# A two-layer decoder step: the first two product tiles grow with the loaded inputs

## The chip, the cores and the metric

The kernel runs on one core of one Trainium2 chip. The metric is device time in microseconds of one execution, as the median of several. Five engines matter: TensorE (PE, with its weight loads shown apart as PEld), VectorE (DVE), ScalarE (ACT), GpSimd (POOL) and SyncE (SP), which here only issues DMAs. A granted clock of 1.00 means that no throttle was recorded.

## The reference

One inference step of a decoder with two layers, for a prompt of 512 tokens with 16 learned tokens ahead of it and for 8 sequences of 8 new tokens: 592 columns of 1024 features, all in float32. The part that the change touches is the very first: the first layer's first RMSNorm and the first product of its feed-forward block.

```python
def rms_norm(x, g):
    y = xf * lax.rsqrt(jnp.mean(xf * xf, axis=-1, keepdims=True) + EPS)
    return (y * g.astype(jnp.float32)).astype(x.dtype)

def swiglu(h, w_gu, w_down):
    g, u = jnp.split(h @ w_gu, 2, axis=-1)
    return (jax.nn.silu(g) * u) @ w_down

def layer(x, lp, ...):
    x = x + 0.5 * swiglu(rms_norm(x, lp['norm_ffn1']), lp['ffn1_w_gu'], lp['ffn1_w_down'])
    m, ... = mixer(rms_norm(x, lp['norm_mix']), ...)      # SSD scan and stick-breaking attention
    x = x + m
    x = x + 0.5 * swiglu(rms_norm(x, lp['norm_ffn2']), lp['ffn2_w_gu'], lp['ffn2_w_down'])
```

`ffn1_w_gu` is 1024 x 5632 (2816 gate columns, then 2816 up columns).

## The kernel before

**How the work is tiled.** The residual stream lies feature by feature: eight tiles `X[0..7]` of 128 features x 592 tokens. A product tile is 128 output features x 592 tokens, held in a pair of PSUM banks of 296 columns each. Both operands are split into a high part of reduced width (float32r) and a low part that holds the rest: weights into `whi` and `wlo`, inputs into `XH` and `XL`. A product tile is then, for each of the eight input tiles and each half, three matmuls: high by high, high by low, low by high. That makes 8 x 2 x 3 = 48 matmuls of 128 x 296.

**The norm.** RMSNorm's factor depends on the token alone, so the gain goes into the split of the inputs (`norm_tile`: `XH = X * gain` on ACT, `XL = X * gain - XH` on DVE), and the factor `R` is multiplied in when a product tile is read from PSUM (`times_r`, L231). `R` needs the squares of all eight tiles. `factor` makes it in steps that run between the matmuls of `mm3`: it is a generator (`flow`), and `step`, called once after each matmul, moves it on by one. With the numbers (8, 0, 20) it lets 8 matmuls pass, puts in the token sums (matmuls of the squares with a column of ones, L476), makes the reciprocal root in small DVE operations, lets 20 more pass, and spreads the result over all partitions with ten small matmuls (L208). Until then `hold` is set, and finished product tiles wait in PSUM, listed in `wait_done`.

**The start.** `setup` loads constants and calls `load_x`. It loads the tokens as rows in two halves of 512 features, with the first weight block (`raw0`, four input tiles x 256 columns) between the halves. For each input tile k it transposes six pieces on PE into a pair of banks (`xps`, 400 and 192 columns), copies them to `X[k]` (400 columns on DVE, 192 on ACT), and calls `norm_tile`, which splits the tile and makes its square: even tiles on POOL, odd ones on ACT. The squares are added into one tile, save the last, on DVE or POOL. Then `ffn` calls `gemm` for two gate tiles, two up tiles, and so on. `gemm` loads weight blocks (`raw`, three buffers), splits each when its product is due (`split`: ACT for the high part, DVE for the low one; three buffers each), and calls `mm3`.

**PSUM.** There are eight banks: three tagged `g`, two `pm`, and one each of `sc`, `po`, `pw`. `bank` deals them out in a cycle, with `turn` as the counter; `WIDE` is g, pm, g, pm, g, sc, and so leaves room for three product tiles. `factor` uses `po` and `pw`.

**Order.** The program text gives priorities; a planner goes through it with modelled durations and writes the order of each engine's instructions, so an instruction that is ready can be put ahead of one that stands before it in the text. In the mixer, hand-written due times (`PRI`, `UNIT`) move groups of instructions further.

Of the kernel before, what the change touches and what calls it, by code (L numbers as in the profile page):

```python
# [8 lines left out]
F32 = mybir.dt.float32  # L9
# [3 lines left out]
AF = mybir.ActivationFunctionType  # L13
ALU = mybir.AluOpType
# [3 lines left out]
D = 1024  # L18
KD = 8
DFF = 2816  # L20
NTOK = 592
# [85 lines left out]
class Kern:  # L107
# [126 lines left out]
    def setup(self):  # L234
        nc, I = self.nc, self.I
        off, arr = self.CA
        w = arr.shape[1]
        call = self.call = self.cst([128, w], "call")
        nc.sync.dma_start(call[:, 0:129], I["c_const"][:, 0:129])
        for k, (o, n) in off.items():  # L240
            setattr(self, "c_" + k, call[:, o:o + n])
        self.ident = self.c_ident
        self.identr = self.cst([128, 128], "identr", F32R)
        nc.vector.tensor_copy(self.identr, self.ident)
        self.flows, self.hold, self.wait_done, self.gn, self.gl, self.gi = [], False, [], "", "", 0
        self.eps = self.cst([128, 1], "eps")
        nc.vector.memset(self.eps, 1e-6)
        self.XH, self.XL = [None] * KD, [None] * KD
        self.cols(0, 296)
        self.par = self.cst([128, 128], "par")  # L250
        self.pcol = {}
        self.params(0, ("norm_ffn1", "norm_mix", "norm_ffn2"))
        self.load_x()
        self.norm_end()

    def params(self, r0, names):

# [130 lines left out]
    def load_x(self):  # L388
        nc, I = self.nc, self.I
        self.xtiles()  # L390
        src = [(I["meta_tokens"], 16, 0)]
        xp = I["x_prompt"][0]
        for b in range(4):
            src.append((xp[b * 128:(b + 1) * 128, :], 128, 16 + 128 * b))
        src.append((I["x_sample"].rearrange("b t d -> (b t) d"), 64, 528))
        toks = [(self.kv.tile([128, 1024], F32, name="xt", tag="kn", bufs=6), n, c) for _, n, c in src]
        for h in range(2):
            for (t, n, _), (s, _, _) in zip(toks, src):
                nc.sync.dma_start(t[0:n, 512 * h:512 * h + 512], s[:, 512 * h:512 * h + 512])
            if h == 0:  # L400
                self.raw0 = self.raw(I["ffn1_w_gu"][0], 0, 4, 0, 256)
        for k in range(KD):
            ps = self.pair("xps")
            for t, n, c in toks:
                o = ps[0][:, c:c + n] if c < 400 else ps[1][:, c - 400:c - 400 + n]
                nc.tensor.transpose(o, t[0:n, k * 128:k * 128 + 128], self.ident[0:n, 0:n])
            nc.vector.tensor_copy(self.X[k][:, 0:400], ps[0][:, 0:400])
            nc.scalar.activation(self.X[k][:, 400:592], ps[1][:, 0:192], AF.Copy)
            if k == 0:
                self.split0 = self.split(self.raw0, 4, 0)  # L410
            self.norm_tile(k, "norm_ffn1", 0, nc.gpsimd if k in (1, 3, 5) else nc.vector,
                           None if k % 2 else nc.gpsimd)

    def store_y(self, h):

# [220 lines left out]
    def gemm(self, src, r0, nk, c0, XH, XL, done, wide=2, after=None):  # L636

        kcs = []
        k = 0
        while k < nk:  # L640
            n = min(4, nk - k)
            kcs.append((k, n))
            k += n
        raws = {}
        if self.gn != self.gl:
            self.gl, self.gi = self.gn, 0
        base = self.gi
        self.gi += wide

        def part(k, n, m, ps):  # L650
            if k not in raws:
                raws[k] = self.raw0 or self.raw(src, r0 + k * 128, n, c0, wide * 128)
                self.raw0 = None
            with self.ahead(None, base + m):
                hi, lo = self.split0 or self.split(raws[k], n, m)
                self.split0 = None
            self.mm3(ps, hi, lo, n, XH[k:], XL[k:], k == 0, k + n == nk, after)

        wait = self.wait_done
        for m in range(wide):  # L660
            ps = self.pair("g")
            for k, n in kcs:
                part(k, n, m, ps)
            wait.append((done, m, ps))
            if not self.hold:
                with self.ahead(None, base + m):
                    for f, i, p in wait:
                        f(i, p)
                wait.clear()
# [977 lines left out]
```

## Time and profile before

| | us |
|---|---|
| runs shown | 2679.93, 2688.82, 2701.83 |
| median | 2688.82 |
| profiled execution | 2681.37 |
| its span | 2679.6 |
| mean granted clock | 0.987 |

The profile is of one execution. Its page names, for each engine, busy time, share of the span and number of instructions; a chain of waits leads back from the last instruction to what released it at each step; a timeline lists instructions with start and duration in us, and in brackets how long the engine had been idle and what ended that. Groups are written "line engine operation out<-in shape xcount | busy us, mean ns of one | idle before". `g` is a product tile, `xps` the transposed inputs, `x` is `X`, `xh` and `xl` its parts, `raw` a weight block, `xt` a block of tokens as loaded, `sq` a square. Ends of matmuls are modelled, so the pace of PE is read from starts.

### The profile page before, as it was taken

To read this page: it belongs to the slowest core of one execution; us is meant where nothing else is said; L and a number is where in the kernel's file an instruction comes from. 1 tells how busy PE (TensorE), PEld (TensorE's weight loads), DVE (VectorE), ACT (ScalarE), POOL (GpSimd) and SP (SyncE) were. 2 spreads that over 40 slices of the span, in tenths; PEclk is the share of its full clock that TensorE was granted. 3 is DMA by queue.
4 is the path that set the end of the run, shared out by engine and by line. 5 is a ranking of instruction groups with operands and counts; after the bars stand their busy time and mean duration, and the time that the engine had idled before them with its cause. 6 is when DMAs were issued, how large, how long until landed. Compare 5 with 4: busy or idle time off the path is not lost.

```text
span 2679.6 us, 51326 instructions
## 1 busy us (share of the span) xinstructions
PE 2600.5 (97%) x21547; PEld 2466.6 (92%) x21547; DVE 1505.1 (56%) x3005; ACT 978.9 (37%) x1771; POOL 304.7 (11%) x288
## 2 busy tenths in 40 slices
PE   8999999999889999999999999999998899999999
PEld 7999999898657999999999999998886579999998
DVE  6434346397886743444554343465878957444444
ACT  3222224256564432222332222233566634223222
POOL 1000000034532100000000000001345411000000
PEclk9999999999989999999999999999998999999999
DMA  3232234467973222222222323244678731222222
GB/s 113 80 115 82 85 113 131 127 214 264 336 241 129 70 81 79 79 79 79 79 79 79 97 85 100 78 151 164 223 253 300 249 128 56 88 86 79 85 89 76
DMA packets 245112, 343.28 MB, mean 128 GB/s; under 512 B 32809, under 2 KB 196721, under 8 KB 244881
## 3 DMA queue, kind: packets, MB, share of 16 engines
q1 hardware_dynamic: 208016, 205.77, 24.7%
q0 software_dynamic: 36864, 134.23, 14.5%
q8 instruction: 169, 2.77, 0.4%
q14 instruction: 63, 0.51, 0.1%
HBM read 320.29 MB, written 19.66 MB: 127 GB/s over the span
## 4 chain that ended last, share of the span: by engine, by line
PE 84%; DVE 7%; issue 3%; ACT 3%; DMA 2%; POOL 1%; SPq 0%; DVEq 0%; POOLq 0%; ACTq 0%
PE g L605 72%; PE v L926 2%; DVE kt L1519 2%; PE po L211 1%; PE sc L211 1%; DMA v<-in_cache_v,vi 1%; DVE st L1298 1%; PE pw L476 1%; DMA kn<-in_cache_k,ki 1%; DVE pst L1298 1%; POOL v L1569 0%; PE z L208 0%; PE z L211 0%; DVE xl L447 0%; DVE wlo L596 0%
## 5 line engine op out<-in xcount | busy, mean ns | idle before, releaser
L605 PE MATMUL g<-xl,whi 128*128 128x296 f32 (+1 forms) x3392 | 1014.6, 299 | 2.7 <-DVE xl L447 2.7
L605 PE MATMUL g<-xh,wlo 128*128 128x296 f32 (+1 forms) x3392 | 1012.9, 299 | 2.0 <-DVE wlo L596 2.0
L605 PE MATMUL g<-xh,whi 128*128 128x296 f32 (+1 forms) x3392 | 1011.1, 299 | 1.5 <-DVE gs L231 1.2
L595 ACT ACTIVATE whi<-raw 128x512 fp32r<-128x512 f32 (+1 forms) x664 | 412.6, 622 | 1323.6 <-PE g L605 1240.5
L596 DVE TENSOR_TENSOR wlo<-raw,whi 128x512 fp32r<-128x512 f32 (+1 forms) x664 | 450.3, 678 | 582.8 <-ACT whi L595 529.7
L605 PEld LDWEIGHTS g<-xl,whi 128*128 128x128 f32 x3392 | 638.6, 188 | 5.6 <-DVE xl L447 3.6
L605 PEld LDWEIGHTS g<-xh,wlo 128*128 128x128 f32 x3392 | 638.7, 188 | 4.3 <-DVE wlo L596 2.5
L605 PEld LDWEIGHTS g<-xh,whi 128*128 128x128 f32 x3392 | 638.7, 188 | 4.0 <-DVE gs L231 1.4
L605 PE MATMUL g<-hl,whi 128*128 128x296 f32 (+1 forms) x1408 | 417.8, 297 | 0.0
L605 PE MATMUL g<-hh,wlo 128*128 128x296 f32 (+1 forms) x1408 | 417.6, 298 | 0.0
L605 PE MATMUL g<-hh,whi 128*128 128x296 f32 (+1 forms) x1408 | 416.7, 298 | 0.0
L1508 POOL DMA_INDIRECT kn<-in_cache_k,ki x128 | 128.3, 1003 | 1657.9 <-PE g L605 934.8
L605 PEld LDWEIGHTS g<-hl,whi 128*128 128x128 f32 x1408 | 265.2, 188 | 0.0
L605 PEld LDWEIGHTS g<-hh,wlo 128*128 128x128 f32 x1408 | 264.3, 188 | 0.0
L605 PEld LDWEIGHTS g<-hh,whi 128*128 128x128 f32 x1408 | 263.9, 188 | 0.0
L1519 DVE STREAM_TRANSPOSE kt<-kn 128x512 f32<-128x512 f32 x256 | 162.9, 681 | 27.7 <-PE sc L211 14.5
L704 DVE SCALAR_TENSOR_TENSOR x<-g,x 128x296 f32<-128x296 f32 (+1 forms) x192 | 88.1, 463 | 119.1 <-PE g L605 118.5
L1569 POOL DMA_INDIRECT v<-in_cache_v,vi x128 | 143.3, 1119 | 100.0 <-DVE kt L1519 36.1
L231 DVE TENSOR_TENSOR us<-g,R 128x296 f32<-128x296 f32 (+1 forms) x176 | 81.5, 464 | 129.1 <-PE g L605 129.0
L231 DVE TENSOR_TENSOR gs<-g,R 128x296 f32<-128x296 f32 (+1 forms) x176 | 80.6, 463 | 126.2 <-PE g L605 121.3
L691 ACT ACTIVATE hh<-us 128x592 fp32r<-128x592 f32 (+1 forms) x88 | 61.2, 696 | 64.3 <-DVE us L689 64.3
L605 PE MATMUL g<-mh,whi 128*128 128x296 f32 (+1 forms) x256 | 77.7, 312 | 2.4 <-ACT mh L1277 1.3
(372 smaller groups left out, 2838.8 us busy)
## 6 DMA issues: line engine op xcount, KB each, us to landing
raw<-in_ffn_w_gu SPq DMA_DIRECT2D x176, 512.0 KB
raw<-in_ffn_w_down SPq DMA_DIRECT2D x80, 512.0 KB
raw<-in_w_in SPq DMA_DIRECT2D x44, 512.0 KB
raw<-in_w_out SPq DMA_DIRECT2D x16, 512.0 KB
spill<-x SPq DMA_DIRECT2D x16, 296.0 KB
x<-spill SPq DMA_DIRECT2D x16, 296.0 KB
raw<-in_ffn_w_down SPq DMA_DIRECT2D x16, 256.0 KB
xt<-in_x_prompt SPq DMA_DIRECT2D x8, 256.0 KB
```

Of the source, the lines that this page charges most:

```text
L211: i = self.nc.tensor.matmul(*a, **k).ins
L231: self.nc.vector.tensor_tensor(tv[0:P, h, :], ps[h][0:P, 0:self.n], rv[0:P, h, :], ALU.mult)
L595: nc.scalar.activation(hi[:, 0:nk], s, AF.Copy)
L596: nc.vector.tensor_tensor(lo[:, 0:nk], s, hi[:, 0:nk].bitcast(F32), ALU.subtract)
L605: mm = nc.tensor.matmul(ps[h][:, 0:self.n], w[:, k, :], self.hv(x)[:, h, :], start=(first and k == 0 and i == 0), stop=(last and k == nk - ...
L691: nc.scalar.activation(hh[:, a:b], u[:, a:b], AF.Copy)
L704: nc.vector.scalar_tensor_tensor(v, p, 0.5, v, ALU.mult, ALU.add)
L926: nc.tensor.matmul(ps[c], x[:, t0:t0 + 128], w.rearrange("p x c -> p (x c)"), start=(k == 0 and i == 0), stop=(k == 7 and i == 2))
L1298: self.nc.vector.tensor_tensor_scan(sv, sv, self.zero[0:rows].to_broadcast([rows, b - a - 1]), 1.0, ALU.mult, ALU.add)
L1508: self.nc.gpsimd.indirect_dma_start(kn, None, self.kflat, bass.IndirectOffsetOnAxis(ap=self.kidx[self.l][:, s, 2 * i + u:2 * i + u + 1], a ...
L1519: self.nc.vector.transpose(kt[:, 2 * u:2 * u + 2].rearrange("p t h i -> p t (h i)"), kns[u][:, :, 256 * quad:256 * quad + 256])
L1569: self.nc.gpsimd.indirect_dma_start(v.rearrange("p k c -> p (k c)"), None, self.vflat, bass.IndirectOffsetOnAxis(ap=self.vidx[self.l][:, s ...
```

## The change

`load_x` builds the first two product tiles itself. It loads both weight blocks of the first gate tiles (`raws`), reserves their PSUM banks (`self.first`: a `pm` and a `g` bank each), and takes only `sc`, `po` and `pw` in turn for the transposed inputs. For each input tile it makes the high part on ACT from `X[k]`, the low part on DVE in two pieces (400 and 192 columns) with PSUM as its source instead of `X[k]`, and then the 12 matmuls of this input tile for both product tiles. The copy of the left 400 columns goes to ACT for odd tiles. Weights are split for both product tiles at once, before input tiles 0 and 4. The squares come after all of that, two on ACT and six on POOL; the sums on DVE gather five of them into the first, so that three square tiles go into the token sums instead of two. `turn` is set to 4. The first call of `gemm` finds the two tiles done and only lists them in `wait_done`; the counted steps of `factor` therefore begin in the third product tile.

```diff
@@ setup
         self.load_x()
-        self.norm_end()
@@ load_x
+        wgu = I["ffn1_w_gu"][0]
         for h in range(2):
             for (t, n, _), (s, _, _) in zip(toks, src):
                 nc.sync.dma_start(t[0:n, 512 * h:512 * h + 512], s[:, 512 * h:512 * h + 512])
             if h == 0:
-                self.raw0 = self.raw(I["ffn1_w_gu"][0], 0, 4, 0, 256)
+                raws = [self.raw(wgu, 0, 4, 0, 256)]
+        raws.append(self.raw(wgu, 512, 4, 0, 256))
+
+        self.first = [self.pair("g", ("g", "pm")) for _ in range(2)]
         for k in range(KD):
-            ps = self.pair("xps")
+            ps = self.pair("xps", ("sc", "po", "pw"))
             for t, n, c in toks:
                 o = ps[0][:, c:c + n] if c < 400 else ps[1][:, c - 400:c - 400 + n]
                 nc.tensor.transpose(o, t[0:n, k * 128:k * 128 + 128], self.ident[0:n, 0:n])
-            nc.vector.tensor_copy(self.X[k][:, 0:400], ps[0][:, 0:400])
-            nc.scalar.activation(self.X[k][:, 400:592], ps[1][:, 0:192], AF.Copy)
-            if k == 0:
-                self.split0 = self.split(self.raw0, 4, 0)
-            self.norm_tile(k, "norm_ffn1", 0, nc.gpsimd if k in (1, 3, 5) else nc.vector,
-                           None if k % 2 else nc.gpsimd)
+            x, gain = self.X[k], self.pcl("norm_ffn1", 0, k)
+            self.XH[k], self.XL[k] = self.half("xh"), self.half("xl")
+            if k % 2:
+                nc.scalar.activation(x[:, 0:400], ps[0][:, 0:400], AF.Copy)
+            else:
+                nc.vector.tensor_copy(x[:, 0:400], ps[0][:, 0:400])
+            nc.scalar.activation(x[:, 400:592], ps[1][:, 0:192], AF.Copy)
+            nc.scalar.activation(self.XH[k], x, AF.Copy, scale=gain)
+            for p, c, n in ((ps[0], 0, 400), (ps[1], 400, 192)):
+                nc.vector.scalar_tensor_tensor(self.XL[k][:, c:c + n], p[:, 0:n], gain,
+                                               self.XH[k][:, c:c + n].bitcast(F32), ALU.mult, ALU.subtract)
+            if k % 4 == 0:
+                w = [self.split(raws[k // 4], 4, m) for m in range(2)]
+            for m in range(2):
+                for h in range(2):
+                    for i, (u, v) in enumerate(((w[m][0], self.XH[k]), (w[m][0], self.XL[k]), (w[m][1], self.XH[k]))):
+                        nc.tensor.matmul(self.first[m][h][:, 0:self.n], u[:, k % 4, :], self.hv(v)[:, h, :],
+                                         start=(k == 0 and i == 0), stop=(k == KD - 1 and i == 2))
+        self.turn = 4
+        sq = []
+        for k in range(KD):
+            s = self.tmp("sq", [128, NTOK])
+            if k in (5, 6):
+                nc.scalar.activation(s, self.X[k], AF.Square)
+            else:
+                nc.gpsimd.tensor_tensor(s, self.X[k], self.X[k], ALU.mult)
+            if k in (0, 6, 7):
+                sq.append(s)
+            else:
+                nc.vector.tensor_tensor(sq[0], sq[0], s, ALU.add)
+        self.factor(sq, 1.0 / D, (8, 0, 20))
@@ gemm
+        if self.first:
+            self.wait_done += [(done, m, ps) for m, ps in enumerate(self.first)]
+            self.first = None
+            return
 ...
-                raws[k] = self.raw0 or self.raw(src, r0 + k * 128, n, c0, wide * 128)
-                self.raw0 = None
+                raws[k] = self.raw(src, r0 + k * 128, n, c0, wide * 128)
             with self.ahead(None, base + m):
-                hi, lo = self.split0 or self.split(raws[k], n, m)
-                self.split0 = None
+                hi, lo = self.split(raws[k], n, m)
```

## The prediction

> **What bounds the kernel now.** The page's first part and its chain say which engine; the windows then say where that engine is not full.
>
> ```profile
> PE 2600.5 (97%) x21547; PEld 2466.6 (92%) x21547; DVE 1505.1 (56%) x3005; ACT 978.9 (37%) x1771; POOL 304.7 (11%) x288
> ```
> ```profile
> 0.00:9.56 9.56, 3.51 (x13) 2.08 (x13) 0.94 (x4) 1.28 (x1) 1.94 (x13) 1.00 0.59 169
> 9.56:18.05 8.49, 7.62 (x34) 5.72 (x35) 7.08 (x10) 7.19 (x17) 4.92 (x4) 1.00 1.07 316
> 18.05:46.04 27.99, 25.29 (x178) 24.15 (x177) 20.92 (x56) 8.98 (x18) 5.57 (x4) 1.00 0.28 78
> 46.04:590.00 543.96, 543.68 (x4141) 532.40 (x4142) 279.02 (x557) 174.45 (x297) 27.26 (x25) 1.00 0.36 111
> 590.00:870.00 280.00, 252.11 (x2887) 200.80 (x2886) 221.22 (x502) 160.10 (x339) 107.11 (x103) 0.95 0.72 248
> ...
> 1760.00:2180.00 420.00, 390.67 (x4025) 328.16 (x4024) 313.99 (x727) 219.56 (x451) 131.41 (x122) 0.96 0.66 223
> ```
>
> Each window row has its bounds and length, then busy time of PE, weight loads, DVE, ACT and POOL. From 46.04 to 590 us PE idles for 0.28 us: whatever the change does to the start, it counts only by how much sooner or later this full stretch begins. So the question is one time: when does the fourth product tile start, 46.04 us now? The change touches nothing behind it but the order in which PSUM banks are dealt. The two mixers idle PE for 27.9 and 29.3 us; they come into a rival.
>
> In the start itself I read PE's timeline for the pace of its work and for its waits (in brackets, with what ended them).
>
> ```profile
> 8.60 7.82 PE L406 MATMUL xps<-call,xt 128*128 128x128 f32 x33 [0.86 <-DMA xt<-in_x_prompt]
> 17.28 1.12 PE L406 MATMUL xps<-call,xt 16*128 16x16 f32 x4 [0.87 <-DVE x L407]
> ...
> 18.45 0.45 PE L605 MATMUL g<-xl,whi 128*128 128x296 f32 x1
> 18.69 0.45 PE L605 MATMUL g<-xh,wlo 128*128 128x296 f32 x1
> ...
> 46.04 0.41 PE L605 MATMUL g<-xh,whi 128*128 128x296 f32 x1 [1.22 <-DVE gs L231]
> ```
> ```profile
> 842.11 1.53 PE L897 MATMUL tm<-call,k 128*128 128x128 f32 x12
> ```
>
> The 33 transposes start (7.82 - 0.43)/32 = 0.231 us apart (0.43 is the mean of one); the 12 of the same shape at 842 us start (1.53 - 0.27)/11 = 0.115 apart. The first products start 0.245 apart. So PE runs at half pace up to about 20.5 us. (The granted clock in the windows says 1.00 there: it doesn't show this.) [...]
>
> The chain of waits gives the rest of the terms:
>
> ```profile
> 35.76 2.13 PE pw L476 x20
> 37.89 5.68 PE g L605 x41
> 43.57 0.06 PE po L208
> ...
> 44.64 0.20 PE g L605
> ...
> 46.04 34.03 PE g L605 x248
> ```
>
> A product at full pace is 34.03/248 = 0.137 us. Before, from 9.56 us (the last full prompt block of the first half lands) the sum is: 35 transposes left of 48 (13 are done) at 0.231 = 8.1; 144 products of three tiles at 0.137 = 19.8; eight of these at half pace, 8 x 0.108 = 0.9; token sums 2.1; the spread of the factor R, 43.57 to 44.64, 1.1; waits 3.6: the 0.87 at 17.28, and 27.99 - 25.29 = 2.70 in the window from 18.05, of which 1.22 are the wait for R at its end. That is 35.6 of the 36.5 us; 0.9 are small gaps.
>
> **The change part by part.** Nothing is taken from the products or the transposes; only their order, the bank plan and the squares change.
>
> *When the first product starts.* Times for it come from ACT, DVE and POOL in the same stretch:
>
> ```profile
> 10.80 0.78 ACT L408 ACTIVATE x<-xps 128x192 f32<-128x192 f32 x3 [8.78 <-PE xps L406]
> 11.45 0.80 ACT L446 ACTIVATE xh<-x,par 128x592 fp32r<-128x592 f32 x1
> 12.13 0.70 ACT L453 ACTIVATE sq<-x 128x592 f32<-128x592 f32 x1
> 12.71 0.64 ACT L595 ACTIVATE whi<-raw 128x512 fp32r<-128x512 f32 x1
> ```
> ```profile
> 12.55 1.59 DVE L447 SCALAR_TENSOR_TENSOR xl<-x,par,xh 128x592 fp32r<-128x592 f32 x1
> 14.07 1.93 DVE L596 TENSOR_TENSOR wlo<-raw,whi 128x512 fp32r<-128x512 f32 x1
> 15.92 0.82 DVE L447 SCALAR_TENSOR_TENSOR xl<-x,par,xh 128x592 fp32r<-128x592 f32 x1
> ...
> 31.11 0.68 DVE L596 TENSOR_TENSOR wlo<-raw,whi 128x512 fp32r<-128x512 f32 x1
> ```
> ```profile
> 11.21 2.30 POOL L451 TENSOR_TENSOR sq<-x 128x592 f32<-128x592 f32 x2 [8.74 <-ACT x L408]
> 13.47 1.97 POOL L459 TENSOR_TENSOR sq<-sq 128x592 f32<-128x592 f32 x1
> ```
> ```profile
> L704 DVE SCALAR_TENSOR_TENSOR x<-g,x 128x296 f32<-128x296 f32 x144 | 66.4, 465 | 86.5 <-PE g L605 86.2
> ```
>
> ```profile
> 10.19 1.63 SPq L586 DMA_DIRECT2D raw<-in_ffn_w_gu  x2
> ```
>
> The loads go out from SP in the order of before: the second weight block, now asked for in the load step, was already the next one behind the inputs (10.19). So the first 192-column copy stays at 10.80. It is then one copy instead of three, the high part can start near 11.1, and the square is no longer between it and the weight's high part: that one ends near 11.1 + 0.8 + 0.6 = 12.5. The first product, 18.05 now, can start at **12.5**. Up to there PE does ten transposes (input tile 0, and the four of tile 1 whose bank is free): 38 are left. Whether the weights had landed by 12.0 isn't shown; bounds are 12.5 and the 12.71 at which they were read, so 0.2 more at most.
>
> *Pace.* From 12.5 products and transposes alternate. I take 4 us at half pace, because 2.4 us, most of them products, raised the clock before and here a third of the time goes to transposes: some 12 products and 8 transposes. Sum: 144 products 19.8, slow ones 12 x 0.108 = 1.3, transposes 8 x 0.231 + 30 x 0.115 = 5.3.
>
> *The wait added.* The inputs' PSUM tiles now use three banks (sc, po, pw) instead of six, and a bank is held until the low part has been read from it. The second bank of tile k+1 is the first of tile k; behind its two transposes, which wait, the products of tile k stand in PE's queue, if the planner puts them there. One round is: two transposes 0.23, the 192-column copy 0.33 (its mean in the trace is 0.330), high part 0.80, first part of the low part. That last operation isn't in the trace; the nearest is the same form on PSUM of 296 columns, 0.465. By column (0.465/296 x 400) it's 0.63 at most, and it is no shorter than 0.465; I take 0.55. With some 0.1 for each of four handovers the round is 2.3 us. PE's own work for a tile is 12 x 0.137 + 6 x 0.115 = 2.33. They are even, so the seven rounds cost little by themselves. But ACT has also two weight splits at the fifth tile, 1.3 us, and the left-hand copies of odd tiles. A second split there waits for one of three buffers, which the products of tile 3 hold. I take **2.0 us of waits**; bounds are 0 (the third tile's second bank is free, and its products can fill the gaps) and 7 x 0.8 = 5.6, if each low part takes the 1.59 us that it took beside POOL instead of 0.82.
>
> ```profile
> L408 ACT ACTIVATE x<-xps x8: 325/330/339, 10.8 to 20.6; 128x192 f32<-128x192 f32 x8
> ```
>
> That POOL work explains 1.59 and 1.93 against 0.82 and 0.68 is read from overlap: POOL works from 11.21 to 15.4. I take the low part as not slowed, being the nearer case: one of its two sources is PSUM now. [...]
>
> *The squares.* They stand behind the splits in the program, but POOL has nothing else at that time, and the planner issues what is ready: I expect them at 11 us again. Six are on POOL (about 1.2 each, by the row at 11.21), two on ACT, five additions on DVE. DVE, 28.0 us busy in the 36.5 from 9.56 on now, gives four copies to ACT and takes two additions from POOL, so it is not the bound on average. What they add to the path is the third square tile in the token sums: 15 calls instead of 10, so 2.13 x 1.5 = **3.2 us, +1.1**. Nothing hides this: PE is the bound. The spread stays 1.1.
>
> ```profile
> 37.93 0.17 DVE L522 TENSOR_SCALAR rv<-pw 128x5 f32<-128x5 f32 x1 [1.11 <-PE pw L476]
> ...
> 40.38 0.17 DVE L529 TENSOR_TENSOR rlo<-ry,rhi 128x5 fp32r<-128x5 f32 x1
> ```
>
> *The wait for R.* Third tile, sums, spread, R, then the first bank freed: as before 1.2 us. The counted steps now begin in the third tile: sums at steps 9 to 23 of it, the spread from step 44. Some 20 products, 2.7 us, cover the chain of small DVE operations that lies between, 2.6 us from its first row to its last; if the squares come late this cover is gone and up to 2.7 us return.
>
> *Sum.* 12.5 + 19.8 + 1.3 + 5.3 + 2.0 + 3.2 + 1.1 + 1.2 = **46.4 us**, against 46.04. What was won (0.87 + 1.48 of waits, 8.1 against 5.8 for transposes) goes into the sums, the new waits, and the hole between 10.7 and 12.5, where before PE transposed three tiles at a time. The change is +0.4 us: the profiled execution (2681.4 us, span 2679.6) would take 2681.8. The median of the runs shown, 2688.8, lies 7.4 above that execution; on its scale the forecast is **2689 us**, no change.
>
> **Rivals.**
> 1. *The front closes up.* The third tile's products fill the new gaps (2.0) and the clock rises after 2.4 us instead of 4 (about 1.0): 43.4 us, 2686. For it: the planner has reordered products before. Against: the first bank of that tile, sc, is held up to the low part of input tile 6.
> 2. *The clock stays down* (the slower side). Products are mixed with transposes, which raised nothing for 8 us. If the mix doesn't count as work, 84 more products cost 0.108 and 30 transposes 0.116 more: 9.1 + 3.5, less the 2.0 of waits that this hides: +10.6 on the sum, 2700 us. [...] Against: before, it rose with 7 products and six transposes around them between 17.28 and 20.48, some 58% of the time products; the mix has 68%. [...]
> 3. *POOL holds DVE up all the same*, at every low part: 5.6 instead of 2.0 us of waits, 50.0 us, 2693. For it: the two slow DVE rows. Against: PSUM as a source.
> 4. *The later order shifts.* The banks' turn is 16 steps behind (4 instead of 20 at the third tile), so in ffn and mixer other banks meet; the planner's due times were set on the old order. Place: the 57.2 us that PE idles in the mixers. A tenth of it either way is 6 us; a half, 29 us, would pass 1%.
> 5. *The change doesn't do what it says*: the planner sets all transposes first. With three banks it can't.
>
> **How the numbers follow.** Forecast (2686 to 2693) 0.55; rival 1, 0.15; 2, 0.10; 3, 0.10; 4, 0.10; rival 5 none. One per cent is 27 us, about what a measurement of this kernel can tell from no change; none of the first three cases reaches it. Of rival 4's 0.10 I give 0.02 to faster by that much and 0.03 to slower, and 0.01 to rival 2 with more on top. Faster 0.02, within 0.94, slower 0.04. The range takes rivals 1 to 3, 2686 to 2700, and the three runs of before, which reach 9 below and 13 above their median: 2677 to 2702.
>
> **What would show it.** First product near 12.5; products 0.245 apart up to about 16.5, then 0.137; transposes after that 0.115; the last product of the eighth input tile near 34; 30 records of token sums in 3.2 us; fourth tile at 46.4, and from there no idle PE. Squares on POOL from 11 us; low parts as two operations of 0.55 and 0.35. I'm wrong if the fourth tile starts before 43 or after 50, or if the mixers' idle time moves by more than 6 us.

## The result, and the profile after

The changed kernel is slower: 2718.0 us (median of 4 runs, 2715.8 to 2724.2) against 2688.2 us for the kernel before, run beside it (4 runs). The ratio is **1.0116, 95% interval 1.0098 to 1.0135**. Forecast were 2689 us, within 2677 to 2702, and no change. The profiled execution of the changed kernel took 2719.7 us with a span of 2717.5, against 2681.4 and 2679.6: 37.9 us more of span.

The page's first part hides it. PE is 97% busy in either kernel:

```profile
PE 2624.6 (97%) x21557; PEld 2478.9 (91%) x21557; DVE 1504.1 (55%) x3011; ACT 982.9 (36%) x1775; POOL 299.1 (11%) x287
```

So I cut both executions where the same work begins and ends: the fourth product tile, the first instruction of the first mixer, the last output product of that mixer, and the same two in the second layer. Each window row has its bounds and length, then busy time of PE, weight loads, DVE, ACT and POOL, the granted clock and the DMA share. First the kernel before, then the changed one:

```profile
522.60:912.00 389.40, 361.23 (x3908) 304.72 (x3905) 313.18 (x708) 214.59 (x443) 133.51 (x124) 0.96 0.66 223
912.00:1851.60 939.60, 937.77 (x6840) 931.14 (x6839) 433.52 (x772) 275.35 (x441) 10.85 (x12) 1.00 0.29 88
1851.60:2243.70 392.10, 360.37 (x3891) 301.71 (x3890) 310.10 (x703) 212.36 (x439) 134.62 (x123) 0.95 0.64 219
```
```profile
53.43:533.50 480.07, 480.07 (x3471) 473.73 (x3472) 221.39 (x416) 139.90 (x226) 7.99 (x9) 1.00 0.32 96
533.50:942.50 409.00, 367.63 (x3890) 305.59 (x3889) 311.90 (x705) 215.71 (x443) 130.25 (x123) 0.94 0.62 210
942.50:1882.50 940.00, 938.51 (x6848) 931.95 (x6847) 435.24 (x772) 275.86 (x441) 13.84 (x12) 1.00 0.29 89
1882.50:2282.60 400.10, 367.95 (x3884) 305.80 (x3883) 309.01 (x702) 211.55 (x438) 132.56 (x122) 0.94 0.63 214
```

Three places, then. The fourth tile starts at 53.43 instead of 46.04 us: **+7.4**. The first mixer takes 409.0 instead of 389.4 us: **+19.6**. The second takes 400.1 instead of 392.1: **+8.0**. Another 3.5 us are lost between the fourth tile and the first mixer (533.5 - 522.6 = 10.9 against 7.4; 1.5 of them are a stretch at half pace at 473 us, shown at the end), and the stretch between the mixers is the same to 0.4 us. In the first mixer PE does the same work (3890 and 3908 records; some are missing from any trace). It idles for 41.4 instead of 28.2 us, which is 13 of the 19.6; the other 6 are a longer busy time, with a granted clock of 0.94 instead of 0.96. In the second mixer PE idles as long as before (32.1 and 31.7 us), so all of its 8.0 us is longer busy time. Over both mixers the trace has 102 us at a granted clock of 0.50 instead of 68 us. At half the clock, those 34 us more cost 17 us at most, which is room for the 14 us of longer busy time.

Who PE waits for in the first mixer is in the waits (from 580 to 912 us, and from 588.1 to 942.5 in the changed kernel), with the time in all, how often, and the longest. The four largest of the kernel before, and the five largest of the changed one ("issue" is a wait for nothing that the profile shows):

```profile
PE sc L208 <- DMA v<-in_cache_v,vi: 4.8, 6, 1.6
PE ph L1197 <- issue: 3.9, 1, 3.9
PE pw L1556 <- ACT wt L1558: 3.1, 2, 1.6
PE pw L1540 <- DVE tot L1537: 2.2, 1, 2.2
```
```profile
PE sc L208 <- DMA v<-in_cache_v,vi: 8.3, 4, 2.9
PE sc L208 <- DVE pst L1328: 3.1, 1, 3.1
PE px L1154 <- ACT dec L1141: 2.8, 2, 2.6
PE zt L1380 <- ACT wt L1588: 2.6, 1, 2.6
PE pY L208 <- DVE xd L1156: 2.5, 2, 1.8
```

The wait for gathered values has grown from 4.8 to 8.3 us. Below it nearly every entry is another: the kernel before has waits of 2 to 4 us too, but other instructions wait. In the changed kernel, several instructions stand at places in PE's queue where their input (a gather, an ACT or a DVE result) is 2 to 3 us late: the order in the queue is another.

**The start**, line by line from PE's timeline of the changed kernel:

```profile
11.79 0.86 PE L426 MATMUL g<-xh,whi 128*128 128x296 f32 x2 [1.76 <-ACT whi L623]
...
19.34 0.40 PE L426 MATMUL g<-xl,whi 128*128 128x296 f32 x1
19.58 0.30 PE L426 MATMUL g<-xh,wlo 128*128 128x296 f32 x1
...
21.65 0.40 PE L426 MATMUL g<-xl,whi 128*128 128x296 f32 x1 [0.19 <-DVE xl L419]
...
22.30 0.47 PE L409 MATMUL xps<-call,xt 128*128 128x128 f32 x2
22.71 0.41 PE L426 MATMUL g<-xl,whi 128*128 128x296 f32 x1
22.95 0.30 PE L426 MATMUL g<-xh,wlo 128*128 128x296 f32 x1
...
26.92 0.41 PE L426 MATMUL g<-xl,whi 128*128 128x296 f32 x1 [2.08 <-DVE xl L419]
...
29.77 0.81 PE L426 MATMUL g<-xh,whi 128*128 128x296 f32 x4 [0.35 <-ACT xh L417]
...
42.98 3.40 PE L504 MATMUL pw<-call,sq 128*128 128x1 f32 x30
...
46.65 0.45 PE L633 MATMUL g<-xh,wlo 128*128 128x296 f32 x1
...
49.61 0.45 PE L633 MATMUL g<-xh,wlo 128*128 128x296 f32 x1
...
53.43 0.40 PE L633 MATMUL g<-xh,whi 128*128 128x296 f32 x1 [1.08 <-DVE gs L231]
```

The terms of the sum against these rows, where 46.4 was forecast and 53.4 measured:

| term | forecast | measured | difference |
|---|---|---|---|
| first product | 12.5 | 11.79 | -0.7 |
| products at half pace up to 19.34 | 12 | 20, x 0.108 | +0.9 |
| waits in the rounds | 2.0 | 0.19 + 2.08 + 0.35 = 2.6 | +0.6 |
| changes between transposes and products | 0 | 0.8 + 3.9 | +4.7 |
| token sums | 3.2 | 3.40 | +0.2 |
| half pace behind the sums | 0 | 13 x 0.108 | +1.4 |
| wait for R | 1.2 | 1.08 | -0.1 |

That is 7.0. The fourth row was not in the sum. From 19.34 to 42.98 are 23.6 us, in which stand 100 products (13.7 at 0.137), 30 transposes (3.45 at 0.115) and the 2.6 of waits: 19.8, so 3.9 are unaccounted for; up to 19.34 it is 7.55 - 20 x 0.245 - 8 x 0.231 = 0.8. The rows at 22.30 show one such change. Two transposes should take 0.23, but the product behind them starts 0.41 later, and the next product 0.24 behind that one instead of 0.137: 0.28 for this change. The trace has 13 changes from transposes to products, 10 of them behind 19.34; at 0.28 these would be 2.8 of the 3.9. The rest stands beside the groups of four transposes and behind the waits, where single steps are 0.05 to 0.10 longer. The second transpose of the pair is a smaller one (64x64), so part of the 0.18 ahead of the product may be due to its shape.

### The profile page after: what moved, and what is told of

Its sections match the earlier page's. It is cut to its first block, busy times and chain, and to the rows that moved or that the text cites. A ratio compares the mean times of both kernels' runs of the same rounds, so it can differ in the third digit from the quotient of the medians.

```text
span 2717.5 us, 51347 instructions
## 1 busy us (share of the span) xinstructions
PE 2624.6 (97%) x21557; PEld 2478.9 (91%) x21557; DVE 1504.1 (55%) x3011; ACT 982.9 (36%) x1775; POOL 299.1 (11%) x287
```

## The experiments

A kernel is called "changed" or "before" by what it was made from; every kernel computes the whole result. Five chips were used after the first comparison, called P to T here in the order in which they come. The kernel before took 2712.3 us (median) on P, 2715.2 on Q, 2687.3 on R, 2684.6 on S and 2688.8 on T, so each ratio is against the kernel before on the same chip.

**1. The phase of the bank counter, and the start, each alone.** `turn` is counted up with each bank that is dealt, and the banks of the mixers' queries and values follow from it modulo 5. The change leaves it 16 behind where the first mixer begins. One kernel is the changed one with the counter put back; the other is the kernel before with the changed kernel's phase, so its start is that of before.

```
changed, in mixer():   +        if l == 0: self.turn += 16
before, in mixer():    +        if l == 0: self.turn += 14
```

> The changed kernel with one line more: at the start of the first mixer the bank counter goes forward by 16, so that the banks are dealt from there on as they were before the change; the start is left as changed. Theory A (the bank turn): some 30 us of the loss come from the phase of the bank cycle, by which the planner orders the mixers otherwise. It expects the fourth tile still at 53.4 us, PE's idle time in the mixers back near 57 us, and 2696 to 2702 us in all, 8 to 13 over before. Theory B (the late start): a start that is 7 us later makes the planner order the mixers otherwise, whatever the banks. It expects no change against the changed kernel: 2714 to 2724 us.

> The kernel before with one line more: at the start of the first mixer the bank counter goes forward by 14, so that the banks are dealt from there on as in the changed kernel. Theory A (the bank turn): the fourth tile stays at 46.0 us, the first mixer takes 15 to 25 us longer, the second 5 to 10, 2708 to 2718 us in all. Theory B (the late start): 2680 to 2700 us, as before.

The start alone: 2722.1 us, ratio **1.0051** (1.0033 to 1.0068). The phase alone: 2720.7 us, **1.0028** (1.0010 to 1.0046), with a fourth tile at 46.09, so its start is that of before. Neither explains 1.0116, and both cost. In the written order of PE's 19,130 instructions, 3864 stand elsewhere (counted from the end) by the phase alone, 1147 by the start alone, and 4045 in the changed kernel. So restoring the counter does not restore the order: the planner reacts to the start as well. It does restore that of the first mixer: of the places that differ by the start alone, fewer than 20 lie there, some 170 in the start and the rest, about 965, in the second mixer. The phase alone moves both mixers.

**2. The same on two other chips.** No edit beyond those of 1; on Q the kernel before, the changed one and both halves.

> The kernel before once more, beside the next three on one chip, with a profile: where its runs stood 24 us higher than the ones shown first (2712 against 2688), the stages tell where. Theory E (the chip): start and feed-forward stages as in the first profile to 1 us, all of the difference in the two mixers, where PE waits for gathered pages and its granted clock falls. Theory F (a general slowing): each stage longer in proportion, 0.9%.

> The changed kernel on the same chip as the next two and as the kernel before. Theory A (the bank turn makes 20 to 30 us of the loss): 1.0 to 1.3% over before, and 0.6 to 1.0% over the next kernel, which has the bank phase of before. Theory G (start alone, the rest differs by chip and run): 0.3 to 0.5% over before, and within 0.2% of the next kernel.

> The changed kernel with the bank phase of before from the first mixer on, again beside the others: 0.3 to 0.5% over before by both theories (its first comparison gave 0.51%).

> The kernel before with the bank phase of the changed one from the first mixer on. Theory A: 0.6 to 1.0% over before. Theory G: within 0.2 of it. (Its first comparison gave 0.28%.) If the phase's cost and the start's cost simply add, this and the run above add up to that of the changed kernel.

On Q: the change 2739.4 us, **1.0088** (1.0061 to 1.0114); start alone 1.0047 (1.0029 to 1.0065); phase alone 1.0033 (1.0014 to 1.0052). There the halves add up to the whole, within their intervals.

Chip S was taken with a kernel that belongs to experiment 5 (two square tiles, counter put back):

> The kernel before, for the stages of the next three on the same chip: mixers of 389 + 392 us if the chip is like that of the first profiles, 401 + 415 if it is like the slow one.

> The changed kernel: 0.9 to 1.2% over before. Theory A (the bank phase makes most of it): the mixers are 15 us or more longer than those of the kernel before on this chip. Theory G (chip and start): under 8.

> The kernel before with the bank phase of the changed one. Theory A: 0.6 to 1.0% over before. Theory G: 0.1 to 0.35%, as on the slow chips.

> The changed kernel with the bank phase of before and two square tiles in the sums. Its start is 4.6 us longer than that of before, and one more stretch at half pace of 1.5 us follows at 471 us. If that is all: 0.15 to 0.3% over before. If a later start costs the mixers something as well: 0.4 to 0.6%, as in the two comparisons with three square tiles.

On S: the change 2730.0 us, **1.0154** (1.0117 to 1.0192); phase alone 1.0047 (1.0029 to 1.0065); the start with two square tiles 1.0019 (1.0000 to 1.0038). The change costs more here than these two together; it has three square tiles, though, so they are not quite its halves. The windows of the first mixer, kernel before and changed kernel on S:

```profile
523.80:922.20 398.40, 371.06 (x3908) 311.56 (x3905) 313.61 (x708) 214.40 (x443) 135.02 (x124) 0.93 0.64 218
```
```profile
533.30:951.00 417.70, 374.63 (x3891) 312.54 (x3889) 311.99 (x705) 216.15 (x443) 129.75 (x123) 0.91 0.61 206
```

+19.3 us, as in the first comparison (+19.6), and PE idles for 43.1 instead of 27.3 us. On Q the first mixer takes 422.6 instead of 401.0 us. What chips share is the place: of the end's +25.9 us on Q and +40.5 on S, 5.9 stand already at the first spill on both (the first store of `X` to memory, in the first layer), and most of the rest comes in the mixers: 17.1 us on Q, where the second mixer is 4.5 us shorter, and 33.4 on S.

**3. Other phases of the counter.** The kernel before, with the counter moved by 6 and by 18.

```
before, in mixer():    +        if l == 0: self.turn += 6        (the other: 18)
```

> The kernel before with the bank counter 6 further from the first mixer on. Steps of 5 in that counter leave the mixers' banks alone, so there are five phases: that of before, that of the changed kernel (14 further, 0.3% slower), this one, the next run's, and one (12 further) that gives the order of before. Theory H (the hand-set due times fit the phase of before): 0.2 to 0.6% over before, with more idle time of PE in the first mixer. Theory I (phases scatter about before): as often faster, -0.3 to +0.3%.

> The kernel before with the bank counter 18 further from the first mixer on, the last of the five phases. Theory H: 0.2 to 0.6% over before. Theory I: -0.3 to +0.3%, with an even chance of its being the fastest kernel of all.

By 6: 2706.9 us, **1.0080** (1.0057 to 1.0104). By 18: 2683.3 us, **0.9981** (0.9965 to 0.9996), the only kernel here that is faster than the kernel before, with an interval that ends just below 1. With nothing but a counter's offset changed, the time spans a whole per cent. The faster one's mixers took 393.6 and 392.6 us in its profile, no less than the 389.4 and 392.1 of before. One profile can't show a gain of 5 us: the second mixer of the kernel before took 392.1, 414.8 and 391.8 us in its three profiles, on three chips. Only the timed runs do.

**4. What the start's rounds cost: the source of the low part, and the banks.** Both are made from the changed kernel with the counter put back, and ran once each on P.

```
-   nc.vector.scalar_tensor_tensor(self.XL[k][:, c:c + n], p[:, 0:n], gain,
+   nc.vector.scalar_tensor_tensor(self.XL[k][:, c:c + n], x[:, c:c + n], gain,

-   ps = self.pair("xps", ("sc", "po", "pw"))
+   ps = self.pair("xps", ("sc", "po", "pw", "g"))
```

> The first experiment (bank phase of before from the first mixer on), with the low parts of the inputs made from the copy in SBUF again instead of from PSUM; a PSUM bank of the start is then free after the copy. Read at the start of the fourth tile, 53.4 us in the changed kernel. Theory C (banks held too long): the rounds of the eight input tiles, 4.2 us each by the starts of the low parts, fall by 1 us or more, and the fourth tile starts 2 to 6 us sooner. Theory D (PE itself: products at half pace and time lost at each change between transposes and products): at most the 2.6 us of waits go, the fourth tile starts at 51 to 53.4; low parts beside squares on POOL may take 1.6 instead of 0.95 us.

> The first experiment, with a fourth PSUM bank for the transposed inputs (a g bank as well as sc, po and pw), so that two whole input tiles fit. Read at the start of the fourth tile. Theory C (banks held too long): the rounds fall below 3.5 us and the fourth tile starts at 48 to 51 us. Theory D (PE itself): the transposes come in larger groups, so fewer changes between the kinds of work, 1 to 2 us at most beside the 2.6 of waits; fourth tile at 50 to 53. Against both: the third product tile's second bank is now taken in turn by the inputs, and its products can't fill gaps.

The fourth tile starts at 50.77 us with the low part read from SBUF and at 49.63 with a fourth bank, against 54.08 for the kernel they are made from: **-3.3 and -4.4**. Part of it is pace: some products in the start begin 0.22 to 0.26 us ahead of the next, at half pace or just behind a change. There are 45 in the kernel that these are made from, 36 with SBUF and 17 with the fourth bank; 9 and 28 fewer are worth 1.0 and 3.0 us. That part is not shown to be the banks': in the first two, 11 to 14 of the slow products stand behind the token sums, in the third none, and experiment 5 finds that this stretch comes and goes with the execution. What is left, 2.3 and 1.4 us, fits a bank that is held until the low part is read. But the kernel with SBUF also has 7 changes from transposes to products instead of 13 (12 with the fourth bank), so its 2.3 us do not part theory C from theory D. The total times of these single runs (2725.4 and 2719.2 us) say nothing of the start: their mixers differ too.

The row of the low parts in the kernel that reads SBUF, and in the changed kernel (DVE's timeline):

```profile
17.66 1.87 DVE L419 SCALAR_TENSOR_TENSOR xl<-x,par,xh 128x400 fp32r<-128x400 f32 x2
...
22.42 0.95 DVE L419 SCALAR_TENSOR_TENSOR xl<-x,par,xh 128x400 fp32r<-128x400 f32 x2
```
```profile
11.26 0.96 DVE L419 SCALAR_TENSOR_TENSOR xl<-xps,par,xh 128x400 fp32r<-128x400 f32 x2 [2.57 <-ACT xh L417]
...
15.53 0.95 DVE L419 SCALAR_TENSOR_TENSOR xl<-xps,par,xh 128x400 fp32r<-128x400 f32 x2
...
20.97 0.95 DVE L419 SCALAR_TENSOR_TENSOR xl<-xps,par,xh 128x400 fp32r<-128x400 f32 x2
21.84 0.16 DVE L312 TENSOR_SCALAR nb<-hp 128x16 f32<-128x16 f32 x1
...
25.54 0.29 DVE L1041 TENSOR_TENSOR dtw<-dtr,dtw 128x32 fp32r<-128x32 f32 x2
...
26.24 0.95 DVE L419 SCALAR_TENSOR_TENSOR xl<-xps,par,xh 128x400 fp32r<-128x400 f32 x2
```

From SBUF the pair takes 1.73 to 1.87 us in the three cases beside POOL's squares, and 0.95 behind them; from PSUM it takes 0.95 throughout, beside POOL too (the pair at 11.26 overlaps a square that ends at 11.65, the one at 40.34 a square that ends at 40.81; in the kernel below, with the low part from PSUM alone, a pair of 0.96 us at 12.31 lies wholly within two squares on POOL, 11.24 to 13.54). So with both inputs in SBUF this operation took about twice as long beside a square on POOL (1.73 to 1.87 against 0.95 us), and with one of them in PSUM no longer than alone (0.95 to 0.96); the second half no row of before had shown. The rows from 21.84 to 25.54 are small setup constants and one addition of squares, which stand ahead of the next low part in DVE's queue. The high part that it reads is done at 23.97 on ACT, so it starts 2.3 us late: this is the wait of 2.08 us at 26.92 on PE.

Then the low part from PSUM alone, in the kernel before (on R), in two pieces as in the change:

```
-   self.norm_tile(k, "norm_ffn1", 0, ..., None if k % 2 else nc.gpsimd)
+   self.norm_tile(k, "norm_ffn1", 0, ..., None if k % 2 else nc.gpsimd, ((ps[0], 0, 400), (ps[1], 400, 192)))
```

> One part of the change alone in the kernel before: the low parts of the loaded inputs come from PSUM, in two pieces. By the rows of the changed kernel the pair takes 0.95 us also beside squares on POOL; from SBUF beside POOL it took 1.6 to 1.9 in the kernel before. Theory J (VectorE is what the start before waits for): the three slow low parts fall by 0.6 to 0.9 us each, the fourth tile starts 1 to 2 us sooner than the 46.0 to 47.8 of before. Theory K (PE is the bound there, the low parts are covered): within 0.5 us. The total within 0.2% of before by both.

2695.5 us, **1.0025** (1.0007 to 1.0044): 6.7 us by the ratio. Both theories named there fell. PE's timeline shows why:

```profile
13.09 1.60 PE L406 MATMUL xps<-call,xt 16*128 16x16 f32 x6 [2.08 <-DVE xl L448]
15.39 4.73 PE L406 MATMUL xps<-call,xt 16*128 16x16 f32 x18 [0.70 <-DVE xl L448]
24.25 1.60 PE L406 MATMUL xps<-call,xt 16*128 16x16 f32 x6 [4.12 <-DVE xl L448]
27.39 0.59 PE L606 MATMUL g<-xh,whi 128*128 128x296 f32 x1 [1.54 <-DVE xl L448]
```

The transposes and the first product now wait for the low parts, 8.4 us in these rows, and the first product comes at 27.39 instead of 18.05. The first spill leaves 6.2 us later than in the profile of before (432.7 against 426.5 us), and the kernel is 6.7 us slower. That agrees with a late start that reaches the end one for one, with mixers of 393 and 391 us. It doesn't show it: the ratio's interval is 1.9 to 11.8 us, and PE's order differs here too, in some 950 places, nearly all of them in the start and the second mixer.

**5. Two square tiles instead of three.** Changed kernel with the counter put back, on R (one run, 2687.6 us, where the kernel before has a median of 2687.3; ten runs on S are in 2):

```
-            if k in (0, 6, 7):
+            if k in (0, 7):
```

> The changed kernel with the bank phase of before from the first mixer on, and two square tiles in the token sums instead of three, as before the change: 20 records instead of 30 there. By the sum of the prediction the fourth tile starts 1.1 us sooner than the 53.2 to 54.1 of its parent. If also the products at half pace behind the sums are due to the length of that stretch of narrow matmuls (3.4 us), they go, and it is 2.6 us sooner.

```profile
42.88 2.29 PE L504 MATMUL pw<-call,sq 128*128 128x1 f32 x20
...
45.24 0.30 PE L633 MATMUL g<-xl,whi 128*128 128x296 f32 x1
```

The fourth tile starts at 50.67, 3.4 earlier than at 54.08. The sums are 1.1 shorter, as the prediction had it, and the products behind them run at full pace. It would be easy to put that down to the shorter sums. Other profiles say no. The kernel before on Q has 20 sums and then this:

```profile
39.34 0.45 PE L605 MATMUL g<-xh,whi 128*128 128x296 f32 x1
```
```profile
39.13:42.53 3.40, 3.40 (x16) 3.40 (x15) 1.70 (x10) 0.63 (x1) 0.00 (x0) 0.50 0.23 83
```

The granted clock in this window is 0.50. So is it behind the sums of the changed kernel:

```profile
46.54:49.93 3.39, 3.39 (x16) 3.39 (x15) 2.12 (x14) 0.00 (x0) 0.00 (x0) 0.50 0.67 221
```

On Q that is half pace from 39.1 to 42.5 us, 14 products, in the same program whose profile in the prediction has none. Some 11 to 15 slow products stand behind the sums in 5 of the 7 profiles with 30 sums and in 6 of the 13 with 20. So this stretch comes and goes with the execution, and the 1.4 us in the table above is no cost of the change. On Q and S, where the kernel before has it too, the first spill of the changed kernel is 5.9 us late instead of the 7.3 of the first comparison.

**6. A late start without the change, and the best phase with the best start.** On T: the kernel before with 30 idle transposes ahead of those of its inputs, and the changed kernel with two square tiles and the phase of the faster kernel of 3.

```
before:   +        slow = self.own("po", [128, 512])
          +        for i in range(30): nc.tensor.transpose(slow[:, 0:128], self.ident, self.ident)
changed:  if k in (0, 7): ...      and in mixer():  +        if l == 0: self.turn += 4
```

> The kernel before with 30 transposes of the unit matrix, whose result nobody reads, ahead of those of the inputs: PE has 7 us more to do at 0.231 each, part of it in its wait for the loads, so the fourth tile should start 3 to 6 us later. Banks and everything else are unchanged, but the planner writes another order in the mixers (858 of 19,129 PE instructions stand elsewhere). Theory L (lateness passes through one to one): 0.1 to 0.25% over before. Theory M (any other order than the one that the due times were set for costs more): 0.4% or more, with the mixers 5 us or more longer than before.

> The changed kernel with two square tiles in the sums and the bank phase of the fastest of the five (18 further than before). If phase and start add: 0.2 to 0.3% for the start less 0.2 for the phase, so -0.1 to +0.15% against before. If the pair gives an order of its own, as in the changed kernel: 0.5% or more over before.

The idle transposes: 2696.0 us, **1.0030** (1.0011 to 1.0049), 8 us, though the fourth tile is at 47.62, no later than on Q and S without them (47.76, 47.27). The first mixer takes 390.5 us in its profile and the second 405.2; 858 of PE's instructions stand elsewhere. So the loss isn't lateness, and with a start that isn't late theory L was not put to the test. What is left is the order: of the 858 places some 770 lie in the second mixer, more than a thousand microseconds behind the 30 instructions. That start isn't late, for one because PE is at full pace sooner:

```profile
2.65 5.24 PE L404 MATMUL po<-call 128*128 128x128 f32 x24 [2.65 <-DMA call<-in_c_const]
...
8.01 0.87 PE L404 MATMUL po<-call 128*128 128x128 f32 x6
```

The first 24 idle transposes begin 0.21 us apart, the last five of the next six 0.11. The other kernel: 2690.1 us, **1.0001** (0.9983 to 1.0018). With a fourth tile at 54.56 it is even with the kernel before: the phase's 0.19% and what the start loses would about cancel. Its profile shows no gain in the mixers (400.5 and 386.1 us, together 786.6, against 786.2 in the faster kernel of 3). In the mixers PE's order is that of the faster kernel of 3, but for a handful of places. So these two differ by the start alone: 1.0001 on T against 0.9981 on R, 0.20%, for a first spill that is 7.2 us later (0.27%). Where the order stays, the start seems to cost no more than its lateness; the two were not run on one chip. No kernel here with the changed start beat the kernel before; the one to keep is that of before with the counter moved by 18.

## Why the prediction was wrong

- **What bounds the kernel: half right.** From 53.43 to the mixers PE idles for nothing, so in that stretch the start counts one for one, as said. But "the change touches nothing behind it but the order in which PSUM banks are dealt" was costed at nothing in the sum. That step failed most: the mixers hold 27.6 of the 37.9 us. And the banks are not all that it touches: with the counter put back, the start alone still changes the order of the second mixer and costs 0.5%.
- **Rival 4, the later order, is the case that came**, with 0.10 of the chance. Its place was right; it was priced at 6 us, a tenth of the 57.2 us of idle time, with half of it, 29 us, as a far end of 0.05. In the mixers as cut here, PE's idle time went from 59.9 to 73.5 us, and the other 14 us came as longer busy time at a lower granted clock (102 us at 0.50 instead of 68), which no share of the idle time could hold.
- **The start: right in mechanism, mis-sized**, +7.4 for +0.4. The first product (11.79 for 12.5), the length of the low part (0.95 for 0.90), the sums (3.40 for 3.2), the spread and the wait for R were right. Mis-sized were the changes between transposes and products (4.7, not in the sum) and the pace (20 slow products for 12, and 13 more behind the sums). Part of the +7.4 is chance: the stretch behind the sums comes and goes, and on Q and S the lateness is 5.9. The round was forecast as 2.3 us by the chain of its operations; the low parts begin 11.26, 15.53, 20.97, 26.24 us, then down to 40.34 for the eighth, (40.34 - 11.26)/7 = 4.15 apart. The 0.1 us for each handover in that chain was an estimate; at the first tile the low part starts 0.04 behind the end of the high part (11.22 to 11.26).
- **Rival 1** came by half: 24 products of the third tile stand between 30.4 and 41.2 us, but they fill time that the changes and the pace had taken. **Rival 3** did not come: from PSUM the low parts take 0.95 us beside POOL's squares too. That they would not be slowed, on which the forecast's 2.0 us of waits rest, no run had shown by then.
- **Rival 2** did not come: full pace came with the mix too, only later, 7.8 us after the first product, not 4. In the ten profiles with the changed start it takes 1.4 to 8.0 us, so the 4 were a guess within a wide spread. That the share of products in the mix (68% against 58%) decides was the author's estimate; no run shows it. The premise, that transposes raise nothing, held in the profile from which it was read, and fails in others. In the kernel with the counter moved by 6, whose start is that of before, full pace is there with the first products:

```profile
8.99 7.68 PE L406 MATMUL xps<-call,xt 128*128 128x128 f32 x33 [1.22 <-DMA xt<-in_x_prompt]
...
18.44 0.30 PE L605 MATMUL g<-xl,whi 128*128 128x296 f32 x1
18.57 0.30 PE L605 MATMUL g<-xh,wlo 128*128 128x296 f32 x1
```

Only transposes had gone before the first product at 18.20; the next ones begin 0.13 us apart. The kernel before with the changed kernel's phase on S shows the same, and so do the idle transposes of 6: in these three, full pace came behind transposes alone.

- **The squares**, expected on POOL from 11 us although they stand behind the splits:

```profile
10.48 1.17 POOL L435 TENSOR_TENSOR sq<-x 128x592 f32<-128x592 f32 x1 [8.00 <-ACT x L416]
...
39.63 1.18 POOL L435 TENSOR_TENSOR sq<-x 128x592 f32<-128x592 f32 x1 [9.97 <-ACT x L416]
```

Each runs as soon as its X is there. Of this part of the change, only the third square tile has a price.

**What stays open.** Shown is that the phase alone costs 0.28 to 0.47%, the start alone about 0.5%, and that other phases of the same kernel lie from -0.19 to +0.80%. The start alone includes another order of the second mixer. Why one order is slow and another fast, instruction by instruction, was not settled. On S, where the start alone with three square tiles was not run, the whole (1.54%) is more than the phase (0.47%) and what the start could cost by its lateness (5.9 us, 0.22%). The changed kernel's order differs from either half's (from the phase alone in 2404 places), so it is one more draw; that this accounts for all of the remainder is argued, not shown. On each of three chips the changed kernel's mixers have more time at a granted clock of 0.50 than those of before (102 us for 68, 113 for 85 on Q, 147 for 92 on S); whether the new order brings this about was not tested.

## What to carry to other kernels

Before costing an edit at the start of a planned program at "the start's microseconds", ask which counters and due times it shifts for later stages: where PE waits, at places in its queue, for gathers and other engines (it idles 41.4 us in the changed kernel's first mixer), a new order alone can move the time by 0.8% (1.0080 with the counter moved by 6), so measure the edit with the counter put back, and try the counter alone; it may be the cheaper gain. Price a mix of transposes and products by its changes (4.7 us here), not only by the two sums, and a bank by how long its last reader holds it (the 2.3 and 1.4 us of experiment 4 fit that, but don't show it). Where a gain or loss of a few microseconds is claimed from two profiles, look first at whether the same stretch differs between two profiles of one kernel.

## What the runs showed of the hardware

- **Half-pace stretches in full work.** Without a gap on PE its products drop to 0.245 us apart for some 3.4 us, and the granted clock to 0.50; here in the changed kernel, far behind the start:

```profile
470.71 2.06 PE L504 MATMUL pw<-call,sq 128*128 128x1 f32 x18
...
473.31 0.45 PE L633 MATMUL g<-xh,wlo 128*128 128x296 f32 x1
...
476.27 0.45 PE L633 MATMUL g<-xh,wlo 128*128 128x296 f32 x1
```
```profile
473.20:476.60 3.40, 3.40 (x16) 3.40 (x15) 1.65 (x10) 1.19 (x3) 0.00 (x0) 0.50 0.18 70
```

14 products, 1.5 us lost. It stands there in 7 of the 10 profiles of kernels made from the changed one, and in none of the 10 made from the kernel before. PE had no gap there; 18 sums of one column had gone before. The same sums stand there in all 20 kernels, so that they bring it about is not shown. The stretches shown here are 3.2 us (46.65 to 49.86 in the changed kernel) to 3.4 us long (473.2 to 476.6). The number of slow products differs between profiles of one start: the start of before has 8 in the first profile and none in that with the counter moved by 6.

- **Full pace behind transposes alone.** In 2 of the 8 profiles with the start of before, PE is at full pace ahead of the first product, behind 33 transposes in a row; in the other 6 it comes 2.3 to 4.4 us behind it. The granted clock reads 1.00 throughout (from 8.6 to 21 us in the first profile, from 8 to 20 in the changed kernel's): it doesn't show this first slow stretch, while it does show the later ones (0.50 from 473.2 to 476.6).
- **A change from a pair of transposes to products** cost PE about 0.28 us at full pace in the changed kernel (0.41 - 0.23 = 0.18 ahead of the first product, 0.24 - 0.137 = 0.10 behind it, in the rows at 22.30).
- **Chips differ by 1.1%** for one kernel (medians 2684.6 to 2715.2 us), and nearly all of it in the mixers: against the first profile, that of the kernel before on Q is 1.7 us late at the first spill, 13.3 at the end of the first mixer, 13.3 at the second layer's first spill, 36.0 behind the second mixer and 36.0 at the end.
